# Opening of a two-sequence encoder layer on one core: inputs transposed on the host, twelve gate/up blocks begun instead of seven, the opening's order written out by hand

## The chip, the cores and the metric

The kernel runs on one core of one Trainium2 chip. The metric is the device time of one execution in microseconds; lower is better. All arithmetic is in fp32; where a matrix product is wanted at fp32 accuracy, the kernel splits each operand into a rounded part ("hi") and its remainder ("lo") and adds three matmuls (hi x hi, hi x lo, lo x hi).

## The reference

Two sequences of 512 tokens, `x_prompt` and `x_sample` (1 x 512 x 1024 each), go through the same encoder layer:

```python
def swiglu(x, w_gate, w_up, w_down):
    return (jax.nn.silu(x @ w_gate) * (x @ w_up)) @ w_down

x = x + 0.5 * swiglu(rms_norm(x, ffn1_norm), ffn1_w_gate, ffn1_w_up, ffn1_w_down)   # 1024 -> 2816 -> 1024
h = rms_norm(x, mix_norm)                  # then attention and mLSTM in parallel, gated, merged
x = x + merged @ w_out
x = x + 0.5 * swiglu(rms_norm(x, ffn2_norm), ffn2_w_gate, ffn2_w_up, ffn2_w_down)
y = rms_norm(x, final_norm)
```

`rms_norm(x, g)` divides each token's row by the root of its mean square and multiplies each column by `g`. The change concerns the first line only: how the first feed-forward (FFN) is begun.

## The kernel before

The two sequences share every weight, so the kernel multiplies both at once by a scheme with seven products where eight would be expected (as Strassen's). For the gate and up matrices of one FFN, the 1024 input columns are halved (lower `l`, upper `u`), and the 2816 outputs are cut into 22 blocks of 128 (`NF`). A block needs seven products, each 12 matmuls of 128x512 (4 slices of 128 input columns x 3 for hi/lo): `B11`, `B21`, `T1`, `T2_`, `T3`, `T4`, `B22`. The right-hand sides of `B11` and `B21` are the lower and upper half of the prompt alone; those of the other five are the sample's upper half and differences of halves of both sequences. The weights' sides are the block's gate weights (`gu_left_a`) and differences of gate and up weights (`gu_left_b`). Each side is split into hi and lo by one ScalarE (ACT) and one VectorE (DVE) instruction (`w_pair`, `put`).

A block can therefore be begun with the prompt alone: `gu_first` multiplies `B11`, copies the partial sum out, adds `B21`, and takes the silu. `Up.begin` does that ahead of time and parks the two results in DRAM (`kept`); `Up.rest` is the loop over all 22 blocks, which fetches parked results back (`resume`) or does `gu_first` itself, and then does the other five products (`gu_rest`). Before, `AHEAD = 7` blocks are begun, and `ORDER` alternates a begun block with one that is not, as long as there are begun ones:

```python
ORDER = [j for p in zip(range(AHEAD), range(AHEAD, NF)) for j in p] + list(range(2 * AHEAD, NF))
```

The opening before is this. Both sequences are loaded as rows (tokens on partitions, `load_x`). `norm_x(0)` squares and sums the prompt's rows on DVE, takes the reciprocal root in eleven small DVE instructions (`rstd_cols`, `rstd_of`), and divides the rows. TensorE then transposes the rows in 32 transposes of 128x128 (`turn`); from PSUM, `first_x` multiplies by the norm's gain `g1` and splits into hi and lo, and `park_x` writes the transposed prompt to DRAM (`xnbuf`) since PSUM and SBUF are wanted. Blocks 0 and 1 are begun, `norm_x(1)` and another 32 transposes do the same for the sample, `sums_of` and `right_sums` make the sums for the other five products, and blocks 2 to 6 are begun among them. Then comes `up.rest`, then the down projection (`ffn_down`).

A planner sets the order of the instructions on each engine from the order of the program and from priorities (`shifted`), except where `pin` (`tc.keep_in_program_order`) holds them in the written order. DMAs of the SP queue are issued in order, each after its own wait.

Of the kernel before, what the change touches and what calls it, by code (L numbers as in the profile page):

```python
# [8 lines left out]
F32 = mybir.dt.float32  # L9
# [17 lines left out]
def encoder(ctx, tc, I, outs):  # L27
# [97 lines left out]
    nc.gpsimd.dma_start(g1, I["ffn1_norm"][0].rearrange("(k p) -> p k", p=P))  # L125


# [5 lines left out]
    warm = cpool.tile([P, 1], F32, name="warm")  # L133
    nc.scalar.activation(warm, ones[:, 0:1], AF.Silu)
# [41 lines left out]
    def rstd_cols(v, width, n):  # L176
        a = rs_tile(width)
        nc.vector.tensor_scalar(a, v, 1.0 / n, EPS, op0=ALU.mult, op1=ALU.add)
        return rstd_of(a, width)

    def col_sums(acc, bs=(0, 1, 2, 3)):
# [4 lines left out]
        nc.vector.tensor_reduce(c, p[:, bs[0] * P:(bs[-1] + 1) * P].rearrange("p (b d) -> p b d", d=P), axis=AX.X,  # L186
                                op=ALU.add)
        return c

    def bcast_psum(r):  # L190

        pr = PT()
        for b in range(4):
            nc.tensor.transpose(pr[:, b * P:(b + 1) * P], r[:, b:b + 1].to_broadcast([P, P]), ident)
        return pr
# [51 lines left out]

    def w_pair(t, src, pin=lambda i: i):
        pin(nc.scalar.activation(t[:, 0], src, AF.Copy))  # L249
        pin(V_.tensor_tensor(t[:, 1], src, f(t[:, 0]), op=ALU.subtract))  # L250
# [13 lines left out]
    def gu_left_b(rg, ru, ring, left):  # L264
# [5 lines left out]
        V_.tensor_tensor(a, u0, u1, op=ALU.add)  # L270
        V_.tensor_tensor(u0, g0, u0, op=ALU.subtract)
        V_.tensor_tensor(g0, a, g0, op=ALU.subtract)
        V_.tensor_tensor(g1_, g1_, g0, op=ALU.subtract)
        wb = w8_tile()
        w_pair(wb, halves(rg))
        left.update({T2_: part(wb, 0), B22: part(wb, 1)})

        def more():
            wd = [v(ring.wd(F32R)) for _ in range(2)]
            split(a, *wd)  # L280
            wc = w8_tile()
            w_pair(wc, halves(ru))
# [3 lines left out]
    def product(p, w, xt, first):  # L286
        wh, wl = w
        for k in range(HK_):
            for i, (a, b) in enumerate(((wh, 0), (wh, 1), (wl, 0))):
                nc.tensor.matmul(p, a[:, k, :], xt[:, b, k, :], start=(first and k == 0 and i == 0),  # L290
                                 stop=(k == HK_ - 1 and i == 2), skip_group_check=True)
# [16 lines left out]
    def gu_rest(W, xc, got, ring, mid):  # L308

        Y, Z = PS(), PT()  # L310
        second = lambda: product(Y, W[T2_], xc[T2_], True)
# [61 lines left out]
    AHEAD = 7  # L373

    ORDER = [j for p in zip(range(AHEAD), range(AHEAD, NF)) for j in p] + list(range(2 * AHEAD, NF))

    class Up:


        def __init__(self, xc, wg, wu, rb):  # L380
            self.xc, self.rb = xc, rb
            self.v = wg, wu
# [13 lines left out]
            r.junk = [r.o.rows[1][:, i] for i in range(2)]  # L396
            r.lone, r.last = lone, fa
# [13 lines left out]
        def rest(self, raw, at=None, hook=None):  # L411
            ring = self.ring

            def resume(j):
                got = ring.v(), ring.h()
                for t, d in zip(got, self.kept.pop(j)):
                    nc.sync.dma_start(t[:, 0], d)
                return got

            left = {}  # L420
            gu_left_b(*raw, ring, left)()
            raw = self.fetch(ORDER[1])
            got = resume(ORDER[0])
            for i, j in enumerate(ORDER):
# [7 lines left out]
                h = gu_rest(W, self.xc, got, ring, lambda: then.append(resume(nxt)) if nxt in self.kept else None)  # L432
# [23 lines left out]
    def ffn_down(wd, rb, ring, tail, xres, done, at_step, hook, ends=None):  # L456
# [19 lines left out]
        def load_raw(fp, i):  # L476
# [3 lines left out]
            fb = ORDER[2 * fp + i]  # L480
# [135 lines left out]
    def mix_gains():  # L616
        pin = tc.keep_in_program_order
        for t, n in ((gm, "mix_norm"), (g2, "ffn2_norm")):
            pin(nc.gpsimd.dma_start(t, I[n][0].rearrange("(k p) -> p k", p=P)))
        pin(nc.gpsimd.dma_start(gbias, I["mlstm_gate_bias"].rearrange("a c -> (a c)").partition_broadcast(P)))  # L620
        pin(nc.gpsimd.dma_start(hn, I["mlstm_head_norm"][0].rearrange("(k p) -> p k", p=P)))
# [529 lines left out]
    raws = [A([P, 4, D], F32, "raw") for _ in range(2)]  # L1151
    xc = [None] * 7
    up = Up(xc, I["ffn1_w_gate"], I["ffn1_w_up"], rbuf[0])
    xins = [I[n][0] for n in ("x_prompt", "x_sample")]

    kept = [[dpool.tile([P, S], F32, name=f"kept{j}_{i}") for i in range(2)] for j in range(AHEAD)]

    def load_x(s):
        for b in range(4):
            nc.sync.dma_start(raws[s][:, b, :], xins[s][b * P:(b + 1) * P, :])  # L1160

    def turn(s, k, banks):
        p = banks[k % len(banks)]()
        for b in range(4):
            nc.tensor.transpose(p[:, b * P:(b + 1) * P], raws[s][:, b, k * P:(k + 1) * P], ident)
        return p
# [31 lines left out]
    def norm_x(s):  # L1198

        sq = [spool.tile([P, 4], F32, tag="cs4", bufs=4, name=nm("cs4")) for _ in range(2)]  # L1200
        junk = up.ring.junk
        for b in range(4):
            for i in range(2):
                x_ = raws[s][:, b, i * S:(i + 1) * S]
                pin(V_.scalar_tensor_tensor(junk[i], x_, 1.0, x_, op0=ALU.mult, op1=ALU.mult,
                                            accum_out=sq[i][:, b:b + 1]))
        pin(V_.tensor_tensor(sq[0], sq[0], sq[1], op=ALU.add))
        rs = rstd_cols(sq[0], 4, D)
        for b in range(4):
            if b % 2:  # L1210
                pin(nc.scalar.activation(raws[s][:, b, :], raws[s][:, b, :], AF.Copy, scale=rs[:, b:b + 1]))
            else:
# [279 lines left out]
```

## Time and profile before

| | |
|---|---|
| time, median of 3 runs | 2116.05 us (2113.82 to 2117.22) |
| profiled execution: its own time | 2115.01 us |
| profiled execution: span from first to last instruction | 2113.2 us |
| granted TensorE clock, mean | 0.996 |
| busy share of TensorE (PE) / its weight loads / DVE / ACT / GpSimd (POOL) | 98% / 80% / 74% / 45% / 5% |
| mean DMA rate | 170 GB/s |

In the profile, PE stands for TensorE's matmuls and PEld for its weight loads, SPq for the queue that issues most DMAs. Times in a timeline start at the span's first instruction. A row of several merged instructions gives the start of the first, the time to the end of the last, and their number; in square brackets stands the idle time of the engine before it and what ended it. Matmuls are pipelined: the pace is the distance of starts, not the duration of one.

### The profile page before, as it was taken

The numbers are of one execution on the slowest core, as the hardware profiler recorded it, in microseconds if no ns is written. First come the engines' busy times: TensorE is split into PE (matmuls) and PEld (weight loads), VectorE is DVE, ScalarE is ACT, GpSimd is POOL, SyncE is SP. The second block draws the span as 40 slices with busy tenths as digits, with TensorE's granted clock in tenths as the row PEclk, the third lists the DMA queues.
The fourth block names the chain that finished last, engine by engine and source line by source line (L and its number), as shares of the span: only waits on it lengthen the run. The fifth ranks groups of instructions, "written<-read, shape, count | busy, mean of one in ns | idle before, by whom it ended". The sixth has DMA issues, their size and how long they took to land.

```text
span 2113.2 us, 26221 instructions
## 1 busy us (share of the span) xinstructions
PE 2070.4 (98%) x9472; PEld 1694.7 (80%) x9472; DVE 1556.0 (74%) x2569; ACT 940.6 (45%) x1568; POOL 97.4 (5%) x106
## 2 busy tenths in 40 slices
PE   7999999999999999999999999999999999999997
PEld 5888888888888777878887787788788888888886
DVE  7888787776796796574649865764887877776687
ACT  6443443442225566463436555544543434343224
POOL 0000000001000110000101101010000000000002
PEclk9999999999999999999999999999999999999999
DMA  7464543389764222232341222344546544369763
GB/s 268 150 222 166 211 179 140 145 323 387 263 230 140 76 75 73 82 117 83 117 159 56 75 91 79 130 156 163 169 154 225 179 169 179 140 245 403 275 212 139
DMA packets 137489, 361.76 MB, mean 171 GB/s; under 512 B 13360, under 2 KB 13376, under 8 KB 136336
## 3 DMA queue, kind: packets, MB, share of 16 engines
q1 hardware_dynamic: 136480, 358.30, 47.7%
q0 software_dynamic: 592, 1.27, 0.3%
q8 instruction: 74, 1.21, 0.2%
q10 hardware_dynamic: 288, 0.52, 0.1%
q14 instruction: 55, 0.45, 0.1%
HBM read 255.15 MB, written 104.89 MB: 170 GB/s over the span
## 4 chain that ended last, share of the span: by engine, by line
PE 85%; DVE 7%; ACT 3%; DMA 3%; issue 1%; SPq 0%; POOL 0%; ACTq 0%; DVEq 0%; POOLq 0%
PE pss L290 17%; PE mm L696 14%; PE pst L290 11%; PE mm L290 10%; PE mm L540 7%; PE mm L680 4%; PE pst L540 4%; PE pss L540 4%; PE mm L1125 3%; PE pso L540 2%; PE pso L952 2%; PE pso L680 1%; PE pss L924 1%; PE pso L1081 1%; PE pss L1032 1%
## 5 line engine op out<-in xcount | busy, mean ns | idle before, releaser
L290 PE MATMUL pss<-xc,w 128*128 128x512 f32 x1584 | 379.4, 390 | 0.7 <-DVE t L320 0.7
L290 PEld LDWEIGHTS pss<-xc,w 128*128 128x128 f32 x1584 | 297.3, 188 | 63.1 <-DVE t L320 1.1
L696 PE MATMUL mm<-xh,w 128*128 128x512 f32 x896 | 293.6, 397 | 0.9 <-DVE w L212 0.9
L290 PE MATMUL mm<-xc,w 128*128 128x512 f32 x1056 | 254.4, 392 | 2.2 <-ACT f L299 2.1
L249 ACT ACTIVATE w<-wr 128x1024 fp32r<-128x1024 f32 x132 | 139.6, 1059 | 236.8 <-PE pst L290 143.6
L290 PEld LDWEIGHTS mm<-xc,w 128*128 128x128 f32 x1056 | 196.9, 188 | 46.3 <-ACT f L299 6.0
L212 DVE TENSOR_TENSOR w<-wr,w 128x1024 fp32r<-128x1024 f32 (+1 forms) x112 | 135.7, 1213 | 116.0 <-ACT w L211 114.9
L250 DVE TENSOR_TENSOR w<-wr,w 128x1024 fp32r<-128x1024 f32 x132 | 161.2, 1223 | 80.5 <-ACT w L249 80.0
L696 PEld LDWEIGHTS mm<-xh,w 128*128 128x128 f32 x896 | 167.8, 189 | 33.6 <-DVE w L212 1.3
L540 PE MATMUL mm<-w,rt 128*128 128x512 f32 x792 | 185.5, 390 | 0.3 <-DMA rt<-rbuf 0.3
L696 PE MATMUL mm<-xl,w 128*128 128x512 f32 x448 | 177.8, 397 | 0.0
L540 PEld LDWEIGHTS mm<-w,rt 128*128 128x128 f32 x792 | 148.5, 188 | 31.4 <-DMA rt<-rbuf 0.7
L211 ACT ACTIVATE w<-wr 128x1024 fp32r<-128x1024 f32 (+1 forms) x112 | 114.6, 1030 | 109.8 <-PE pso L1125 35.0
L290 PE MATMUL pst<-xc,f 128*128 128x512 f32 x528 | 127.2, 389 | 0.0
L290 PE MATMUL pst<-xc,w 128*128 128x512 f32 x528 | 127.0, 389 | 0.0
L290 PEld LDWEIGHTS pst<-xc,w 128*128 128x128 f32 x528 | 99.1, 188 | 20.6
L290 PEld LDWEIGHTS pst<-xc,f 128*128 128x128 f32 x528 | 99.1, 188 | 20.5
L600 ACT ACTIVATE w<-t 128x512 fp32r<-128x512 f32 x82 | 51.6, 631 | 121.9 <-PE pst L540 63.7
L600 ACT ACTIVATE w<-wr 128x512 fp32r<-128x512 f32 x72 | 44.7, 631 | 129.1 <-PE pso L540 65.5
L696 PEld LDWEIGHTS mm<-xl,w 128*128 128x128 f32 x448 | 84.7, 189 | 16.0
L540 PE MATMUL pss<-w,rt 128*128 128x512 f32 x396 | 95.3, 390 | 0.9 <-ACT w L600 0.9
L540 PE MATMUL pst<-w,rt 128*128 128x512 f32 x396 | 94.3, 389 | 0.0
(344 smaller groups left out, 3496.2 us busy)
## 6 DMA issues: line engine op xcount, KB each, us to landing
rt<-rbuf SPq DMA_DIRECT2D x154, 512.0 KB, 6.1
rbuf<-t SPq DMA_DIRECT2D x72, 512.0 KB, 3.2
wr<-in_ffn_w_gate_dram SPq DMA_DIRECT2D x56, 512.0 KB, 4.1
wr<-in_w_in_cols_dram SPq DMA_DIRECT2D x56, 512.0 KB, 3.5
wr<-in_ffn_w_up_dram SPq DMA_DIRECT2D x44, 512.0 KB, 3.5
rbuf<-f SPq DMA_DIRECT2D x30, 512.0 KB, 3.1
rbuf<-tab SPq DMA_DIRECT2D x30, 512.0 KB, 3.7
wr<-in_ffn_w_down_dram SPq DMA_DIRECT2D x48, 256.0 KB, 7.4
```

The costliest lines, as they stand in the source:

```text
L211: pin(nc.scalar.activation(hi, raw, AF.Copy))
L212: pin(lo_eng.tensor_tensor(lo, raw, f(hi), op=ALU.subtract))
L249: pin(nc.scalar.activation(t[:, 0], src, AF.Copy))
L250: pin(V_.tensor_tensor(t[:, 1], src, f(t[:, 0]), op=ALU.subtract))
L290: nc.tensor.matmul(p, a[:, k, :], xt[:, b, k, :], start=(first and k == 0 and i == 0), stop=(k == HK_ - 1 and i == 2), skip_group_check=True)
L540: nc.tensor.matmul(p, r[:, b, d * P:(d + 1) * P], u[:, a, :], start=(first and q == 0 and k == 0), stop=(q == len(us) - 1 and k == 2), ski ...
L600: nc.scalar.activation(hi, src, AF.Copy)
L680: nc.tensor.matmul(p[b][:, :N], a[:, k, bs], w_[:, kl, :], start=(k == 0 and i == 0), stop=(k == KD - 1 and i == 2))
L696: nc.tensor.matmul(p, a[:, k, :], b, start=(k == 0 and i == 0), stop=(k == n - 1 and i == 2))
L924: nc.tensor.matmul(p, qT[:, h, b * P:(b + 1) * P], kv[:, hk * 2 + j, :], start=(j == 0), stop=(j == 1))
L952: nc.tensor.matmul(po, Vst[:, kv_, hk, :], w, start=(kv_ == 0 and i == 0), stop=(kv_ == 3 and i == 1))
L1125: nc.tensor.matmul(p[b], a[:, k, bs], w_[:, k - k0, :], start=(k == 0 and i == 0), stop=(k == KD - 1 and i == 2))
```

## The change

The host hands the kernel each input twice: as rows, as before, and transposed (`x_prompt_t`, `x_sample_t`, 128 partitions x 8 slices x 512 tokens); the four norm gains that lie along partitions are laid out on the host too, as 128 rows. The 64 transposes of the opening and the trip of the prompt through `xnbuf` are gone there (the second FFN keeps its own `sums_of`).

Twelve blocks are begun in the first FFN, seven in the second (`RAW, AHEAD = 6, (12, 7)`). A token's divisor is the same for all input columns, so it can be applied after a product as well: blocks 0 to 5 are begun on the prompt times gain, not divided ("raw"), and their two results are multiplied on DVE by `R[0]`, a 128x512 tile that holds each token's reciprocal root in all partitions (`end`). Meanwhile the rows are squared and summed on ACT (`squares`), rooted on DVE (`root`), and spread over the partitions by four small TensorE transposes (`spread`). Then `normed` divides the transposed prompt, and blocks 6 to 11 are begun on it as before. The sample is divided likewise, half on DVE and half on POOL (`normed1`). Blocks come in pairs: the lower halves (`lower`) of two blocks, then their upper halves (`upper`); `evac` copies the partial sum out between the two.

Everything up to the first product of the loop is pinned in written order on every engine and on the SP queue; the first slice of the prompt goes over ACT's DMA queue. In the loop, the order is 0, 12, 1, 13, ... 9, 21, 10, 11, and the first block's weights are made in the opening.

```diff
-    g1 = ...; nc.gpsimd.dma_start(g1, I["ffn1_norm"][0].rearrange("(k p) -> p k", p=P))
...
-    AHEAD = 7
-    ORDER = [j for p in zip(range(AHEAD), range(AHEAD, NF)) for j in p] + list(range(2 * AHEAD, NF))
+    RAW, AHEAD = 6, (12, 7)
+    def order_of(ahead):
+        return [j for p in zip(range(ahead), range(ahead, NF)) for j in p] + (
+            list(range(2 * ahead, NF)) or list(range(NF - ahead, ahead)))
...
-    load_x(0)
-    raw0 = up.fetch(0, (0,))
-    load_x(1)
-    raw1 = [up.fetch(j, (0,))[0] for j in (1, 2)]
-    norm_x(0)
-    W = [gu_left_a(raw0[0], pin)]
...
-    for k in range(KD - 1):
-        first_x(k)
-    park_x(0)
-    first_x(KD - 1)
-    W.append(gu_left_a(raw1[0], pin))
-    up.begin(0, W[0])
-    for k in range(1, KD):
-        park_x(k)
-    up.begin(1, W[1])
-    norm_x(1)
...
+    load_x(0, 0, 1, nc.scalar)
+    load_half(0, 0)
+    pin(nc.sync.dma_start(g1, I["ffn1_norm"]))
...
+    load_x(0, 1, 2)
+    load_x(0, 2, 4)
+    load_half(1, 0)
+    load_half(0, 1)
+    load_x(0, 4, 6)
+    load_x(0, 6, 8)
+    load_half(1, 1)
+    raws = {2: fetch_next(2)}
+    load_rows(0, (0, 1))
+    raws[3] = fetch_next(3)
+    load_rows(0, (2, 3))
...
+    def split_x(k):
+        t, kk, g, x = xr[k // HK_], k % HK_, g1[:, k:k + 1], x_t[0][:, k, :]
+        pin(nc.scalar.activation(t[:, 0, kk, :], x, AF.Copy, scale=g))
+        pin(V_.scalar_tensor_tensor(t[:, 1, kk, :], x, g, f(t[:, 0, kk, :]), op0=ALU.mult, op1=ALU.subtract))
+    def squares(s, b):
+        v = in_rows[:, b, :]
+        pin(nc.scalar.activation(v, v, AF.Square, accum_out=row_sq[s][:, b:b + 1]))
+    def root(s):
+        return rstd_cols(row_sq[s], 4, D, pin)
+    def spread(s, r):
+        pin(nc.scalar.activation(R[s], bcast_psum(r, pin), AF.Copy))
+    def normed(ks):
+        for k in ks:
+            x = x_t[0][:, k, :]
+            pin(V_.scalar_tensor_tensor(x, x, g1[:, k:k + 1], R[0], op0=ALU.mult, op1=ALU.mult))
...
+    def end(j):
+        X, v1 = begun.pop(j)
+        up.kept[j] = kept[j]
+        if j < RAW:
+            g0 = gate_rows()
+            pin(V_.tensor_tensor(g0, X, R[0], op=ALU.mult))
+            pin(V_.tensor_tensor(v1, v1, R[0], op=ALU.mult))
+            pin(nc.scalar.activation(g0, g0, AF.Silu))
+            pin(nc.sync.dma_start(kept[j][0], v1))
+        else:
+            g0 = part_rows()
+            pin(nc.scalar.activation(g0, X, AF.Silu))
+        pin(nc.sync.dma_start(kept[j][1], g0))
...
+    first_left(0, 0)
+    for k in range(HK_):
+        split_x(k)
+    lower(0)
+    first_left(1, 0)
+    first_left(0, 1)
+    split_x(4)
+    split_x(5)
+    evac(0)
+    lower(1)
+    split_x(6)
+    split_x(7)
+    first_left(1, 1)
+    upper(0)
+    evac(1)
+    upper(1)
+    left(2)
+    squares(0, 0)
+    squares(0, 1)
+    left(3)
+    lower(2)
+    squares(0, 2)
+    squares(0, 3)
+    lower(3)
+    evac(2)
+    fetch_more(4, 5)
+    for k in range(0, KD, 2):
+        load_x(1, k, k + 2)
+    fetch_more(6, 7)
+    load_rows(1, range(4))
+    left(4)
+    r = root(0)
+    upper(2, (0, 1))
+    evac(3)
+    spread(0, r)
+    upper(2, (2, 3))
+    upper(3)
+    left(5)
+    fetch_more(8, 9)
+    normed(range(4))
+    lower(4)
+    lower(5)
+    hi_all(B11, x0l)
+    lo6 = left_hi(6)
+    end(0)
+    evac(4)
+    normed(range(4, 8))
+    hi_all(B21, x0u)
+    upper(4)
...
+    lower(10)
+    lower(11)
+    evac(10)
+    more = gu_left_b(*raw0, rings, W0, pin)
+    hi_all(T1, x0l)
+    upper(10)
+    evac(11)
+    upper(11)
+    lo_all(T1, x0l)
+    more()
+    end(10)
+    end(11)
+    pin(V_.tensor_tensor(x1l, x1u, x1l, op=ALU.subtract))
+    both(T3, x1l)
+    sum2(t4s, lambda i: two(x0u, i), lambda i: t2s[i])
+    both(B22, x1u)
+    both2(T4, t4s)
...
-    tail = up.rest(raw0, 13, mix_gains)
+    tail = up.rest(raw0, 13, mix_gains, W0)
...
+    for n in ("prompt", "sample"):          # on the host
+        x = given[f"x_{n}"][0]
+        given[f"x_{n}_t"] = np.ascontiguousarray(x.T.reshape(KD, P, S).transpose(1, 0, 2))
+    for name in ("ffn1_norm", "mix_norm", "ffn2_norm", "mlstm_head_norm"):
+        given[name] = np.ascontiguousarray(given[name][0].reshape(-1, P).T)
```

More of the change, by code (lines that the diff above doesn't have):

```diff
@@ new lines, in encoder @@
+    first_left(0, 0)
+    for k in range(HK_):
+        split_x(k)
[24 more added lines that the diff above has]
+        load_x(1, k, k + 2)
@@ new lines, in encoder @@
+    squares(1, 0)
+    squares(1, 1)
+    squares(1, 2)
+    lo8 = left_hi(8)
+    squares(1, 3)
+    end(1)
+    lower(6)
+    lower(7)
+    evac(6)
+    end(2)
+    lo8()
+    gain1(range(HK_, KD))
+    lo9 = left_hi(9)
+    evac(7)
+    r = root(1)
+    end(3)
+    upper(6, (0, 1))
+    spread(1, r)
+    lo9()
+    normed1()
+    upper(6, (2, 3))
+    upper(7)
+    end(4)
+    end(6)
+    lo10 = left_hi(10)
+    pin(V_.tensor_tensor(x0l, x1l, x0l, op=ALU.subtract))
+    lower(8)
+    end(7)
@@ new lines, in encoder @@
+    lower(9)
+    lo10()
+    evac(8)
+    upper(8)
+    lo11 = left_hi(11)
+    evac(9)
+    upper(9)
+    end(5)
+    lo11()
+    raw0 = up.fetch(up.order[0])
+    sum2(t2s, lambda i: two(x1u, i), lambda i: two(x0l, i))
+    end(8)
+    W0 = {}
+    both2(T2_, t2s)
+    end(9)
+    lower(10)
[11 more added lines that the diff above has]
+    pin(V_.tensor_tensor(x1l, x1u, x1l, op=ALU.subtract))
```

234 lines of the change are left out of this document (141 added, 93 removed).

## The prediction

> **What bounds the kernel now.** I read the page first, for where TensorE stands still.
>
> ```profile
> PE 2070.4 (98%) x9472; PEld 1694.7 (80%) x9472; DVE 1556.0 (74%) x2569; ACT 940.6 (45%) x1568; POOL 97.4 (5%) x106
> PE   7999999999999999999999999999999999999997
> ```
>
> TensorE is busy 98% of the span, so 43 us is all the idle time there is. The first slice of 53 us, one of two that are not full, is where the change lies. So I asked for the opening by windows, with the loop behind it.
>
> ```profile
> 0.00:10.00 10.00, 3.78 (x16) 3.49 (x16) 4.12 (x14) 1.49 (x2) 4.84 (x11) 1.00 0.81 224
> 10.00:20.00 10.00, 4.39 (x23) 4.16 (x24) 6.82 (x21) 5.29 (x7) 0.23 (x1) 1.00 1.01 394
> 20.00:30.00 10.00, 9.21 (x46) 7.38 (x45) 9.91 (x21) 9.55 (x17) 0.00 (x0) 1.00 0.53 209
> 30.00:40.00 10.00, 7.07 (x32) 5.79 (x31) 7.91 (x25) 5.52 (x7) 0.00 (x0) 0.83 0.90 312
> 40.00:450.00 410.00, 410.00 (x1817) 339.17 (x1816) 330.66 (x412) 177.30 (x231) 0.00 (x0) 1.00 0.51 183
> ```
>
> The columns are PE, PEld, DVE, ACT and POOL busy, granted clock, DMA share and GB/s. After 40 us TensorE is full to 450 us (410.00 of 410), with DVE at 81%. Before that 15.5 us are idle, and part of the busy time is not products. What the opening costs in all comes from TensorE's timeline.
>
> ```profile
> 15.61 0.78 PE L1165 MATMUL pss<-ident,raw 128*128 128x128 f32 x2 [10.79 <-DVE raw L1213]
> 17.46 1.06 PE L1165 MATMUL pss<-ident,raw 128*128 128x128 f32 x4
> 19.17 1.14 PE L1165 MATMUL mm<-ident,raw 128*128 128x128 f32 x8
> 20.50 2.57 PE L290 MATMUL mm<-xc,w 128*128 128x512 f32 x10
> 23.25 0.71 PE L290 MATMUL mm<-xc,w 128*128 128x512 f32 x2
> 24.76 5.76 PE L290 MATMUL mm<-xc,w 128*128 128x512 f32 x24 [0.79 <-ACT f L299]
> 31.25 3.03 PE L290 MATMUL mm<-xc,w 128*128 128x512 f32 x12 [0.73 <-ACT f L299]
> 36.48 0.48 PE L1165 MATMUL pss<-ident,raw 128*128 128x128 f32 x1 [2.20 <-DVE raw L1213]
> 39.81 3.46 PE L290 MATMUL mm<-xc,w 128*128 128x512 f32 x14
> 44.12 3.02 PE L290 MATMUL mm<-xc,w 128*128 128x512 f32 x12
> 47.55 13.99 PE L290 MATMUL mm<-xc,w 128*128 128x512 f32 x60
> 61.37 0.62 PE L290 MATMUL pss<-xc,w 128*128 128x512 f32 x2
> 77.48 2.88 PE L290 MATMUL pst<-xc,w 128*128 128x512 f32 x12
> 80.20 2.88 PE L290 MATMUL pss<-xc,w 128*128 128x512 f32 x12
> ```
>
> The pace of products is (80.20 - 77.48)/12 = 0.2267 us. Until 61.37, 10 + 2 + 24 + 12 + 14 + 12 + 60 = 134 matmuls of products were started, worth 30.4 us. So 61.37 - 30.4 = 31.0 us of the opening brought no product: the wait for the rows' norm, 64 transposes, the second norm. The change leaves the number of products alone (22 blocks x 84 matmuls = 1848, or 419 us at this pace), so the difference in time is the difference in this lost time, as long as TensorE stays full afterwards.
>
> **The change part by part: the lost time after it.** The price rows for the other engines:
>
> ```profile
> 0.72 1.82 SPq L1160 DMA_DIRECT2D raw<-in_x_prompt_dram  x4
> 1.24 1.10 POOL L125 DMA_DIRECT2D g<-in_ffn_norm_dram  x1 [0.81 <-POOLq L1479]
> 4.29 0.69 DVE L1205 SCALAR_TENSOR_TENSOR tab<-raw 128x512 f32<-128x512 f32 x1 [3.29 <-DMA raw<-in_x_prompt_dram]
> 12.52 0.17 DVE L178 TENSOR_SCALAR rs<-cs 128x4 f32<-128x4 f32 x1
> 14.71 2.19 ACT L1211 ACTIVATE raw<-raw,rs 128x1024 f32<-128x1024 f32 x2 [12.49 <-DVE rs L173]
> 17.75 0.66 ACT L1228 ACTIVATE xc<-pss,g 128x512 fp32r<-128x512 f32 x1
> 18.32 0.67 ACT L1228 ACTIVATE xc<-pst,g 128x512 fp32r<-128x512 f32 x1
> 19.02 0.75 DVE L1229 SCALAR_TENSOR_TENSOR xc<-pss,g,xc 128x512 fp32r<-128x512 f32 x1
> 19.68 0.74 DVE L1229 SCALAR_TENSOR_TENSOR xc<-pst,g,xc 128x512 fp32r<-128x512 f32 x1
> 24.12 0.59 ACT L299 ACTIVATE f<-mm 128x512 f32<-128x512 f32 x1
> ```
>
> ```profile
> L249 ACT ACTIVATE w<-wr 128x1024 fp32r<-128x1024 f32 x132 | 139.6, 1059 | 236.8 <-PE pst L290 143.6
> L250 DVE TENSOR_TENSOR w<-wr,w 128x1024 fp32r<-128x1024 f32 x132 | 161.2, 1223 | 80.5 <-ACT w L249 80.0
> ```
>
> *First product: 5.5 us.* The first 512 KB of the prompt, issued at 0.72, were there at 4.29. After the change the first 512 KB are one prompt slice (ACT's queue) and half of block 0's weights (SP's), so 4.3 again. ACT splits the half weight and the slice at 0.57 to 0.6 each: first matmul at 5.5. The norm, the transposes and `xnbuf` are on nobody's path now.
>
> *First product held by DVE: 0.5.* DVE makes five lo parts at 0.66 (19.02 to 19.68), from 4.95 to 8.3, and two matmuls follow: 8.7 instead of 5.5 + 2.7 = 8.2.
>
> *Clock: 2.1.* Four transposes from 17.46 to 18.31 came at 0.21 each, but eight from 19.17 at 0.14: TensorE had been still for 10.8 us and reached its pace some 3.5 us after it began at 15.61. The same pace of 0.21 returned where the record grants 0.54:
>
> ```profile
> 8.00:10.00 2.00, 0.00 (x0) 0.00 (x0) 1.31 (x4) 0.00 (x0) 0.00 (x0) 1.00 1.05 202
> 12.00:14.00 2.00, 0.00 (x0) 0.00 (x0) 1.69 (x11) 0.00 (x0) 0.23 (x1) 1.00 1.03 416
> 18.00:20.00 2.00, 2.00 (x14) 2.00 (x13) 2.00 (x3) 2.00 (x4) 0.00 (x0) 1.00 1.01 403
> 38.00:40.00 2.00, 2.00 (x12) 2.00 (x11) 1.16 (x2) 2.00 (x3) 0.00 (x0) 0.54 0.87 311
> ```
>
> (The 1.00 ahead of the first row is then no grant, only the absence of a record.) No row shows a slow 128x512; I estimate twice 0.2267. If the full clock comes 5 us after the first product, at 10.5, the twelfth matmul starts near 10.4 and ends the product at 10.8 instead of 8.7. Bounds: 0 (full clock from the start) and 3.5 (3 us later still). The Trainium skill, "TensorE: Matmul & The Clock Gate", Part 1, says that the clock runs at half until a free-running window of about 3.4 us has been busy throughout. By that alone full clock comes 3.4 to 6.8 us after 5.5, which makes this term 1.4 to 3.2. The transposes' 3.5 us agree.
>
> *First spread: 1.1.* TensorE reaches the four transposes of `spread` 18 matmuls after `lower(2)` (12 of `lower(3)`, 6 of `upper(2)`), or 4.1 us. In that time runs a chain that `lower(2)` starts, since ACT and DVE go in written order: `evac(2)` 0.6, `left(4)` on ACT 1.06, on DVE 1.22, then `root`, eleven small instructions, 14.71 - 12.52 = 2.2: 5.1, and handovers, 5.2. So TensorE waits 1.1 wherever it stands. Queued behind it are `upper(2)`'s second half and all later products; on DVE `normed`, whose cover is the four raw blocks still to multiply. Bounds 0.5 to 3.5: `squares` needs the prompt's rows, the last of 6 MiB on the queue. At 403 GB/s these land at 4.3 + 5.77 MB/403 = 18.6, and two squares and a weight split later ACT is free by 21, before `lower(2)` is over: the slack is 1 to 2 us, and below about 360 GB/s this wait grows.
>
> *Second spread: 0.* `root(1)` comes after `squares(1)`, whose rows are there by 4.3 + 12.1 MB/403 = 34.3, and before TensorE arrives: 174 matmuls after 10 us of losses, near 50.
>
> *Eight spread transposes:* at 0.14, 1.1, against 64 removed.
>
> *Other waits: 0.4.* DVE has about 40 instructions of 512 columns (0.66), 21 of 1024 (1.22; the 2048-wide ones count twice) and two roots (4.4) ahead of `T2_`: 56 us of the 71 up to 76 us. So the engine isn't the bound; a late handover costs 0 to 4, and I take 0.4, near the timeline's small waits (0.73, 0.79).
>
> *The loop: 0.* TensorE needs (1848 - 288) x 0.2267 = 354 us for what was 381. DVE had 81% of 381 = 307; five more blocks are begun, so five splits of 1.22 leave the loop: 301 of 354, 85%. The cover is thinner, not gone. Ten more fetches of 256 KB go at a DMA share of 0.51. The last pair (10, 11) has two begun blocks, 27.2 us of TensorE against 26 of DVE: the tightest place, price 0 to 2.
>
> *Gains on POOL's queue:* later and contiguous, needed only after the loop: 0.
>
> Sum: 5.5 + 0.5 + 2.1 + 1.1 + 1.1 + 0.4 = 10.7 lost, instead of 31.0: 20.3 saved. The profiled execution's own time is 2115.0 (span 2113.2 and 1.8 around it), so 2094.7; the median of the runs is 1.0 above that execution: 2096.
>
> **The rivals.** *The queue is too slow (slower).* Ahead of the second loop block's weights, SP's queue carries 20.75 MiB, 21.8 MB: both sequences twice (8), twelve gate blocks (6), four loop weights (2), nineteen parked results (4.75). They are wanted by 78 us; that is 287 GB/s from 2 us on. Everything is pinned, so a late piece stops ACT or DVE and, behind it, every product. Pure loads made 403 to 416 (against); mixed with stores, 312 at a DMA share of 0.90, so some 347 (against, with little to spare); but 202 at 8 to 10 us (for), with the small gain DMAs in flight that POOL issued from 1.24 on and that are gone here. At 202 the list ends at 110 us, 32 late: 2128. It decides below 287, and at 227 the gain is gone. The Trainium skill, "DMA: Bandwidth & Descriptors", asks for transfers of 1 MiB or more (section "Measured (HBM→SBUF, 128 partitions, SWDGE, issued from GpSimd)") and gives a single one 2.0 us plus its bytes at 436 GB/s ("Anatomy of one DMA", for POOL's path); one at a time, pieces of 512 KB would by that make 164 GB/s and 2151. The rows of 403 and 416, of such pieces with several in flight, speak against it.
>
> *The clock falls back.* The record's 0.54 came right after 2.2 us of idle time (36.48). If the waits at the first spread and at 5 us do the same, another 3.4 us at half pace: 1.7 each, 2098 to 2100.
>
> *DVE is late at `T3`.* After `T2_`'s sides DVE still has T1's lo, a weight and a 2048-wide difference, T3's lo and smaller ones, 11.7 us, against 7.7 us of products that don't need them (T2_, T1, ten matmuls). It leads by some 4 us when `T2_` starts; without the lead, 4 us are lost: 2100.
>
> *The change doesn't do what it says* is excluded by the built order: the 64 transposes are gone, the products stand in the written order (chance 0).
>
> **How the numbers follow.** The forecast (2091 to 2099): 0.72. Low end: no clock term, no wait at the spread, 3.6 less than 10.7, and half a microsecond from an earlier landing: 2091. The clock falling back: 0.08, DVE late: 0.05, the queue at 255 to 285 GB/s (up to 10 late): 0.07; together 2099 to 2107, 0.20. The queue lower: 0.08, of which 0.03 still faster, 0.02 within 0.2% (4.2 us, about what a measurement can tell from no change), 0.03 slower. Faster 0.95, same 0.02, slower 0.03; range 2091 to 2107.
>
> **What would show it.** Right: first product at 5 to 6 us; block 0's twelve matmuls over 4 to 5.5 us; about 1 us of idle time at `spread` for DVE's `root`, none at the second; the first `T2_` matmul 288 x 0.2267 + 10 to 11 = 75 to 77 us in; TensorE full until the down projection. Wrong: idle time before `upper` or `lower` that ends with a DMA landing or with ACT after one; a DMA rate under 300 GB/s at a full share in the first 70 us; new waits in the loop.

## The result, and the profile after

| | before | after |
|---|---|---|
| median of the runs compared | 2114.94 us (2113.54 to 2117.22, 4 runs) | 2098.03 us (2094.34 to 2100.79, 4 runs) |
| profiled execution: time / span | 2115.01 / 2113.2 us | 2100.79 / 2099.0 us |

The ratio is 0.9918, with a 95% interval of 0.9899 to 0.9937: faster by 17 us. The forecast was 2096 us (2091 to 2107), so the time is 2 us above it. The direction and most of the size were right, but the profile shows that one step of the sum was not.

TensorE's busy share by slices, from the page of the kernel after:

```profile
PE   9999999999999999999999999999999999999997
```

The first digit of TensorE's line went from 7 to 9: the opening is where the time came from. The windows of the kernel after, with the columns as before (PE, PEld, DVE, ACT, POOL busy, granted clock, DMA share, GB/s):

```profile
0.00:10.00 10.00, 7.03 (x24) 5.46 (x25) 3.66 (x8) 5.57 (x9) 0.68 (x6) 0.92 0.77 250
10.00:20.00 10.00, 10.00 (x42) 8.16 (x41) 6.64 (x10) 9.26 (x15) 0.00 (x0) 0.91 1.03 412
20.00:30.00 10.00, 9.02 (x43) 7.24 (x42) 3.46 (x13) 5.06 (x9) 0.00 (x0) 1.00 1.03 411
30.00:40.00 10.00, 10.00 (x45) 8.06 (x44) 9.91 (x13) 6.06 (x7) 0.00 (x0) 1.00 0.87 345
40.00:50.00 10.00, 10.00 (x46) 8.29 (x45) 9.66 (x20) 10.00 (x18) 0.00 (x0) 1.00 0.60 208
50.00:60.00 10.00, 10.00 (x48) 8.23 (x47) 9.74 (x10) 3.49 (x7) 7.20 (x5) 1.00 0.63 215
60.00:70.00 10.00, 8.13 (x29) 6.19 (x29) 9.65 (x10) 7.07 (x11) 2.97 (x5) 0.83 0.86 264
70.00:80.00 10.00, 9.70 (x43) 7.73 (x42) 8.42 (x10) 6.22 (x9) 0.00 (x0) 1.00 0.64 239
80.00:430.00 350.00, 350.00 (x1545) 289.33 (x1544) 299.71 (x382) 146.85 (x187) 0.00 (x0) 1.00 0.58 202
```

Two things stand out. From 60 to 70 us TensorE is idle for 1.9 us and the granted clock is 0.83, in a stretch for which the forecast had no loss. And DVE, with 13.8 us of work in the first 30 us, is then busy for 39.0 of 40.

TensorE's timeline of the kernel after, up to the first matmul of `T2_` (the one at 80.98), and the start of the down projection:

```profile
6.24 0.50 PE L289 MATMUL mm<-xc,w 128*128 128x512 f32 x1 [1.42 <-ACT xc L1245]
22.64 2.88 PE L289 MATMUL pso<-xc,w 128*128 128x512 f32 x12
25.36 1.52 PE L289 MATMUL mm<-xc,w 128*128 128x512 f32 x6
27.86 0.62 PE L189 MATMUL pst<-ident,rs 128*128 128x128 f32 x4 [0.98 <-DVE rs L168]
28.24 1.63 PE L289 MATMUL mm<-xc,w 128*128 128x512 f32 x6
50.30 0.60 PE L189 MATMUL pst<-ident,rs 128*128 128x128 f32 x4
57.56 2.88 PE L289 MATMUL pso<-xc,w 128*128 128x512 f32 x12
62.31 4.61 PE L289 MATMUL mm<-xc,w 128*128 128x512 f32 x12 [1.87 <-ACT t L1281]
66.76 2.91 PE L289 MATMUL pso<-xc,w 128*128 128x512 f32 x12
69.50 8.32 PE L289 MATMUL mm<-xc,w 128*128 128x512 f32 x36
78.13 3.02 PE L289 MATMUL mm<-xc,w 128*128 128x512 f32 x12 [0.30 <-ACT f L1281]
80.98 2.88 PE L289 MATMUL pss<-xc,w 128*128 128x512 f32 x12
434.91 1.30 PE L543 MATMUL mm<-w,rt 128*128 128x512 f32 x5
```

The start of the down projection in the kernel before:

```profile
450.12 2.20 PE L540 MATMUL mm<-w,rt 128*128 128x512 f32 x9
```

The twelve begun blocks have 24 matmuls each. These 288 matmuls at 0.2267 us are 65.3 us, so 80.98 - 65.3 = 15.7 us were lost ahead of the loop, where 10.7 were forecast and 31.0 were lost before. The down projection began at 450.12 before and begins at 434.91 now: 15.2 us saved, and the loop kept them.

Most of the 5 us that are missing stands at one place. The twelve matmuls at 62.31 (`upper(8)`) could have started at 57.56 + 2.72 = 60.28. They started 2.0 us later, and then took 4.45 us (62.31 to 66.76) instead of 2.72, 1.7 more, because the record grants half the clock for 3.4 us from 62.9 on. Another 0.5 us is lost ahead of 78.13. TensorE waited for ACT's `evac(8)`. What ACT waited for before that, by the waits of the kernel after (total, times, longest):

```profile
ACT tab L1295 <- DVE tab L1293: 7.1, 2, 6.5
```

ACT stood 6.5 us in `end(4)`, behind DVE. In the written order three other ACT operations stand between `end(4)`'s silu and `evac(8)`. What DVE did at that time, by its timeline in the kernel after:

```profile
52.75 5.84 DVE L1344 SCALAR_TENSOR_TENSOR xt<-xt,g,tab 128x512 f32<-128x512 f32 x4 [0.26 <-ACT tab L1256]
58.52 0.68 DVE L1293 TENSOR_TENSOR tab<-pss,t 128x512 f32<-128x512 f32 x1
59.12 1.18 DVE L1294 TENSOR_TENSOR t<-t,t 128x512 f32<-128x512 f32 x1
```

POOL's timeline:

```profile
52.80 6.94 POOL L1347 TENSOR_TENSOR xt<-xt,tab 128x512 f32<-128x512 f32 x4 [51.51 <-ACT tab L1256]
```

DVE's groups from 30 to 66 us (busy us, mean ns of one):

```profile
L1344 DVE SCALAR_TENSOR_TENSOR xt<-xt,g,tab 128x512 f32<-128x512 f32 x4 | 5.8, 1519 | 0.3 <-ACT tab L1256 0.3
L1261 DVE SCALAR_TENSOR_TENSOR xt<-xt,g,t 128x512 f32<-128x512 f32 x8 | 5.5, 747 | 0.0
```

L1344 and L1261 are the same operation on tiles of the same shape. L1261 (`normed`, nothing beside it) takes 747 ns; L1344 (`normed1`, beside POOL's L1347) takes 1519 on average and as a group 5.84 us instead of 2.73. That is 3.1 us by which DVE reaches `end(4)` late. L1293, which takes one operand from PSUM, was not slower beside POOL (0.68); L1294, with both operands in SBUF, was (1.18 instead of 0.68), though it reads neither of the tiles that POOL reads. ACT has a smaller part: it puts the gains on POOL's four slices (`gain1`, 2.56 us) ahead of the copy that hands DVE the spread root, and DVE waited 0.26 us for that copy.

So the theory: *POOL's half of `normed1` slows DVE's half; ACT, in its written order, stands behind DVE, and TensorE behind ACT; the clock falls back behind that wait.* The rivals: DVE is slow there for another reason (its operands, transfers that land); ACT is late by its own work; the losses at the start (clock, spread) matter more.

### The profile page after: what moved, and what is told of

Its sections match the earlier page's. It is cut to its first block, busy times and chain, and to the rows that moved or that the text cites. A ratio compares the mean times of both kernels' runs of the same rounds, so it can differ in the third digit from the quotient of the medians.

```text
span 2099.0 us, 26135 instructions
## 1 busy us (share of the span) xinstructions
PE 2064.2 (98%) x9416; PEld 1687.8 (80%) x9416; DVE 1567.0 (75%) x2554; ACT 942.4 (45%) x1571; POOL 106.6 (5%) x109
## 4 chain that ended last, share of the span: by engine, by line
PE 89%; DVE 6%; ACT 3%; DMA 1%; issue 1%; POOL 0%; SPq 0%; ACTq 0%; DVEq 0%; POOLq 0%
PE pss L289 18%; PE mm L699 15%; PE pst L289 11%; PE mm L289 9%; PE mm L543 8%; PE pst L543 4%; PE pss L543 4%; PE mm L683 4%; PE mm L1128 3%; PE pso L543 3%; PE pso L955 2%; PE pso L683 1%; PE pss L927 1%; PE pso L1084 1%; PE pss L1035 1%; PE pso L1128 1%
## 5 line engine op out<-in xcount | busy, mean ns | idle before, releaser
L289 PE MATMUL pss<-xc,w 128*128 128x512 f32 x1632 | 389.4, 389 | 0.0
L289 PEld LDWEIGHTS pss<-xc,w 128*128 128x128 f32 x1632 | 306.1, 188 | 64.3 <-ACT t L1281 0.3
L248 ACT ACTIVATE w<-wr 128x1024 fp32r<-128x1024 f32 (+1 forms) x129 | 134.8, 1046 | 245.0 <-PE pst L289 131.4
L289 PE MATMUL mm<-xc,w 128*128 128x512 f32 x960 | 234.2, 395 | 4.7 <-ACT t L1281 1.9
L207 DVE TENSOR_TENSOR w<-wr,w 128x1024 fp32r<-128x1024 f32 (+1 forms) x112 | 136.3, 1218 | 116.6 <-ACT w L206 116.0
L289 PEld LDWEIGHTS mm<-xc,w 128*128 128x128 f32 x960 | 181.2, 190 | 46.8 <-ACT f L298 2.9
L249 DVE TENSOR_TENSOR w<-wr,w 128x1024 fp32r<-128x1024 f32 (+1 forms) x129 | 155.5, 1206 | 81.7 <-ACT w L248 81.2
L206 ACT ACTIVATE w<-wr 128x1024 fp32r<-128x1024 f32 (+1 forms) x112 | 114.6, 1030 | 110.2 <-PE pso L1128 35.0
```

Of the source, the lines that this page charges most:

```text
L206: pin(nc.scalar.activation(hi, raw, AF.Copy))
L207: pin(lo_eng.tensor_tensor(lo, raw, f(hi), op=ALU.subtract))
L289: pin(nc.tensor.matmul(p, a[:, k, :], xt[:, b, k, :], start=(first and k == 0 and i == 0), stop=(k == HK_ - 1 and i == 2), skip_group_chec ...
```

## The experiments

The wait that some expectations place at "the fifth divided block" is the one ahead of `upper(8)`; the one that they place at the end of the opening, at 77 us, is the wait of `upper(11)` for `evac(11)`.

**The changed kernel again.** No edit.

> The changed kernel again, unaltered, on the same chip as the runs beside it. Expected 2096 to 2100 us, as in the result (2094.3 to 2100.8 there). If the spread there came from whether the clock's fall-back at 62.9 us happens in an execution, a profile of a shorter execution shows full clock at 62 to 66 us, or a shorter wait ahead of it; if the spread has nothing to do with that stall, the profile shows the stall of about 2 us and the clock at half behind it at any length.

2099.60 us (2097.20 to 2100.32, 5 runs), ratio 0.9925 [0.9913, 0.9938]. The same wait of 1.84 us at 62.86 and the same 4.5 us for the twelve matmuls behind it, `T2_` from 81.50 on. The wait is a property of the kernel, not of one execution. The profiled execution was again the slowest of its runs, so it doesn't tell what makes the spread among them.

**`normed1` on DVE alone.**

```diff
-    def normed1():
-        for k in range(HK_):
+    def normed1(ks=range(KD)):
+        for k in ks:
...
-        for k in range(HK_, KD):
-            x = x_t[1][:, k, :]
-            pin(G_.tensor_tensor(x, x, R[1], op=ALU.mult))
...
-    gain1(range(HK_, KD))
```

> The second sequence's normalisation wholly on VectorE: all eight slices there, GpSimd's four products and the gains that ScalarE put on them are gone. Theory (VectorE's 128x512 operations took 1.77 us instead of 0.75 because GpSimd read and wrote beside them): the eight take 0.75 each, 6 us, so VectorE, though it has twice the work, is through at about 58.7 us, as it was with half of it; the wait of 2 us ahead of the fifth divided block's lower product stays within 1 us of that, and the time within 2 us of the changed kernel's. Rival (the operations are slow for another reason: their operands, the transfers that land beside them): they stay at 1.5 to 1.8 us, the eight take 12 to 14, VectorE is 6 to 8 us later and the kernel 4 to 8 us slower than the changed one.

2095.62 us (2095.06 to 2096.22), 4.0 less than the changed kernel beside it. DVE's group from 30 to 66 us:

```profile
L1344 DVE SCALAR_TENSOR_TENSOR xt<-xt,g,tab 128x512 f32<-128x512 f32 x8 | 5.4, 747 | 0.0
```

TensorE's timeline:

```profile
61.26 3.02 PE L289 MATMUL mm<-xc,w 128*128 128x512 f32 x12 [1.03 <-ACT t L1281]
78.57 2.88 PE L289 MATMUL pss<-xc,w 128*128 128x512 f32 x12
```

Eight divisions alone take 5.4 us, less than four beside POOL (5.84), so the rival of other operands or landings falls. The time went further than expected ("within 2 us"): the wait shrank from 1.87 to 1.03 us, and no half clock followed it. Only about half of these 0.84 us is the contention. The divisions end 0.46 us sooner for their duration, and they begin some 0.4 us sooner after the second spread (52.14 - 50.08 against 52.75 - 50.30), because the edit also takes `gain1` off ACT. The down projection starts at 432.63, against 434.91 and 435.45 in the two executions of the changed kernel: 2.3 to 2.8 us earlier. What the medians show beyond that arose later.

**The upper half of `normed1` later.** The edit above, and:

```diff
-    normed1()
+    normed1(range(HK_))
...
     raw0 = up.fetch(up.order[0])
+    normed1(range(HK_, KD))
     sum2(t2s, lambda i: two(x1u, i), lambda i: two(x0l, i))
```

> As the run with the normalisation wholly on VectorE, and the upper four slices are divided later, just ahead of the difference that first needs them. Theory (contention with GpSimd, and ScalarE waiting for VectorE in the written order, made the wait of 2 us and the half clock of 1.7 us behind it): VectorE leaves the first four slices at about 55.8 us instead of 58.6, the wait ahead of the fifth divided block and the half clock at 62.9 to 66.3 us go, 3 to 3.7 us faster than the changed kernel beside it; 3 us of work come later on VectorE, so a wait of up to 2.4 us can come back at the last two lower products, which leaves 1 to 2 us of gain. Rival (ScalarE is late by its own work, VectorE's lateness is only beside it): the wait stays at 1.9 us and the time within 0.5 us.

2097.73 us (2097.15 to 2100.26). TensorE's timeline:

```profile
60.13 2.88 PE L289 MATMUL mm<-xc,w 128*128 128x512 f32 x12
76.26 4.50 PE L289 MATMUL mm<-xc,w 128*128 128x512 f32 x12 [2.37 <-ACT f L1281]
```

The wait at `upper(8)` is gone, without half clock; the one at `evac(11)` came back at its full 2.4 us with a half clock behind it (4.33 us to the next product). Both as expected, and so is the gain, 1.9 us less than the changed kernel beside it. ACT's silu in `end(4)` now waits 3.87 us for DVE instead of 6.51. So it was DVE that made ACT late; ACT's own work had no more than the 0.4 us above, since `gain1` is gone here too.

**Also `evac(11)` ahead of the next weight split.** The two edits above, and:

```diff
     evac(10)
-    more = gu_left_b(*raw0, rings, W0, pin)
     hi_all(T1, x0l)
-    upper(10)
     evac(11)
+    more = gu_left_b(*raw0, rings, W0, pin)
+    upper(10)
     upper(11)
```

> As the run before it (upper four slices divided on VectorE, later), and ScalarE evicts the last begun block ahead of the next block's weight split, which is put behind it, with the last two upper products later. Theory: both waits at the end of the opening are gone, the first product of the second loop pair's operand starts at 77 to 78 us instead of 81, and the kernel is 3 to 5 us faster than the changed kernel beside it. Rival (the loop has no room for what is put off: the weight split and the upper slices come later): the first loop product is early, but waits of 2 to 4 us show in the first loop blocks, and the time is within 1 us of the changed kernel's.

2096.39 us (2094.49 to 2097.07), 3.2 less than the changed kernel. Both waits are gone. TensorE's timeline:

```profile
24.32 2.88 PE L289 MATMUL pso<-xc,w 128*128 128x512 f32 x12
67.40 11.04 PE L289 MATMUL mm<-xc,w 128*128 128x512 f32 x48
78.28 2.88 PE L289 MATMUL pss<-xc,w 128*128 128x512 f32 x12
```

`T2_` begins at 78.28, later than it would have, since in this execution the first 60 matmuls (five half products) lasted until 24.32 instead of 22.64: the half clock lasted 6.8 us there instead of 3.4. The rival has a part too: two waits for DVE appear in the loop, of 0.60 us at 84.94 and of 0.69 at 95.16. From `T2_` to the down projection 355.9 us pass instead of 353.9, so the down projection starts only 0.7 to 1.3 us earlier than in the changed kernel (434.19).

**Longer warm-up.** `for _ in range(8)` becomes `range(11)`: 22 warm-up matmuls instead of 16.

> The changed kernel with 22 warm-up matmuls of 128 columns instead of 16 ahead of the first product (11 passes of two instead of 8), so that TensorE stands still for less than the 1.2 to 1.4 us it does there. Theory (the loss of 2.8 to 4.8 us between the first product's start and the end of the first five half products is the clock, and which window of 3.4 us is busy throughout depends on its phase): full clock comes from the first product on in more executions, the 60 matmuls take 14.5 to 16.5 us instead of 16.4 to 18.4, the kernel is 0 to 2 us faster. Rival (these matmuls wait for VectorE's and ScalarE's splits of late slices, whatever the clock): the 60 matmuls take the same 16.4 or more and the time is the same.

2098.20 us (2097.91 to 2098.64). TensorE's timeline:

```profile
5.97 0.56 PE L289 MATMUL mm<-xc,w 128*128 128x512 f32 x1
21.35 2.88 PE L289 MATMUL pso<-xc,w 128*128 128x512 f32 x12
61.05 3.06 PE L289 MATMUL mm<-xc,w 128*128 128x512 f32 x12 [1.88 <-ACT t L1281]
77.49 4.61 PE L289 MATMUL mm<-xc,w 128*128 128x512 f32 x12 [2.50 <-ACT f L1281]
81.94 2.90 PE L289 MATMUL pss<-xc,w 128*128 128x512 f32 x12
```

The first 60 matmuls took 15.4 us instead of 16.4, with no half clock among them, so the forecast's clock term is real. Yet `T2_` starts no earlier (81.94), and the time is that of the changed kernel (its ratio to the kernel before is 0.9919; the changed kernel's were 0.9918 and 0.9925). The lead of 1.3 us was still there behind the first wait for ACT (61.05 against 62.31), and no half clock followed that wait. All of it was lost at the second wait, 2.50 us for `evac(11)`, and at the half clock behind it.

**The gains on the host, in the kernel before.** The kernel before, with `g1` on SP's queue and all four gains contiguous.

> The kernel before, with only the four gains laid out on the host: the first on SyncE's queue, the others contiguous on GpSimd's queue. Theory of the prediction's queue rival (the 202 GB/s at 8 to 10 us came from the small gain transfers in flight): the rate at 4 to 10 us rises towards 400, the prompt's last rows land 2 to 3 us sooner, the norm and all behind it with them, 2 to 3 us faster than before (ratio 0.9986 to 0.9990). Rival (the transfers start slowly whatever is small beside them): the rate at 8 to 10 us stays near 200 and the time within 0.5 us.

2115.10 us (2112.80 to 2118.43); ratio 1.0000 [0.9991, 1.0009]. Windows of this kernel:

```profile
6.00:8.00 2.00, 0.00 (x0) 0.00 (x0) 1.49 (x6) 0.00 (x0) 0.00 (x0) 1.00 1.08 228
8.00:10.00 2.00, 0.00 (x0) 0.00 (x0) 0.82 (x3) 0.00 (x0) 0.40 (x1) 1.00 0.92 351
```

At 8 to 10 us the rate rose from 202 to 351 GB/s, but the dip only moved, to 228 at 6 to 8 us. Expected was 2 to 3 us; it was nothing that can be measured. The scattered gains did not cause the slow start, and this part of the change is worth nothing by itself.

**The prompt's root ahead of block 4's weight.** `r = root(0)` is written ahead of `left(4)`.

> The changed kernel with the prompt's root written ahead of block 4's weight split instead of behind it. Prediction's step (TensorE waits 1.1 us at the first spread because evacuation, weight split and root follow one another on VectorE): the wait of 1.0 us ahead of the first spread goes, 1 us earlier from there on; the weight of block 4 comes 2.2 us later and is not wanted before 18 matmuls more. The time is 1 us less if nothing later waits for another reason, and up to 0.5 us less if VectorE's lateness at the fifth divided block (which does not change) takes the rest back. Rival (the squares, so the queue, are what comes late): the wait stays.

2099.12 us (2097.40 to 2099.91). TensorE's timeline:

```profile
26.84 1.52 PE L289 MATMUL mm<-xc,w 128*128 128x512 f32 x6
28.20 0.60 PE L189 MATMUL pst<-ident,rs 128*128 128x128 f32 x4
78.51 4.61 PE L289 MATMUL mm<-xc,w 128*128 128x512 f32 x12 [1.95 <-ACT f L1281]
```

The wait of 1.0 us at the first spread is gone (26.84 + 6 x 0.2267 = 28.20), so it was the order on DVE, as forecast, and not the rows' transfers. The time is the changed kernel's (ratio 0.9921). Two things took the gain: in this execution the half clock at the start lasted longer (the first 60 matmuls took 18.1 us instead of 16.4), and `evac(11)` was waited for again, with half clock behind it.

**Seven blocks begun instead of twelve.** `RAW, AHEAD = 6, (7, 7)`, and what blocks 7 to 11 did in the opening left to the loop.

> The changed kernel with seven blocks begun in the first feed-forward network instead of twelve: six on undivided input and one on divided input; blocks 7 to 11 are left to the loop. Theory (the twelve blocks are the cover for VectorE's opening; without five of them TensorE stands still until the first difference of the four input quarters is made): 120 matmuls, 27 us, less cover, 5 weight splits and evictions less on VectorE and ScalarE, so a wait of 15 to 20 us ahead of the first loop product, 2112 to 2120 us, which is the kernel before again. Rival (VectorE's opening is mostly the work of the blocks themselves): the wait is under 8 us and the time under 2106.

2120.68 us (2118.58 to 2123.97); ratio 1.0024 [1.0014, 1.0033], slower than before. TensorE's waits:

```profile
PE pss L289 <- ACT w L248: 20.9, 1, 20.9
```

One wait of 20.9 us, ahead of the first `T2_` product; expected were 15 to 20, and 2112 to 2120 us. The five more blocks are the cover for DVE's opening. The same early start, without them, gains nothing at all.

**All four edits together** (sample's division on DVE in two halves, `evac(11)` early, root early, 22 warm-up matmuls).

> Four edits of the changed kernel together: the sample's normalisation wholly on VectorE with its upper half later, the last eviction ahead of the weight split, the prompt's root ahead of block 4's weight split, 22 warm-up matmuls. Theory (each of the last two brought TensorE 1 us or more forward and lost it again to the two waits of ScalarE for VectorE and SyncE's queue at 61 and 77 us; with those waits gone it is kept): first loop product at 73.5 to 76 us, 9 to 10.5 us lost ahead of it, 2092 to 2095 us, 3 to 6 us faster than the changed kernel. Rival (the waits at 61 and 77 us are the limit of all the opening's work on VectorE, so what is brought forward is lost again in another wait): first loop product at 77 us or later, and the time that of the run with the first two edits, 2096.

2095.82 us (2094.33 to 2097.17). TensorE's timeline:

```profile
75.73 2.88 PE L289 MATMUL pss<-xc,w 128*128 128x512 f32 x12
431.81 6.28 PE L543 MATMUL mm<-w,rt 128*128 128x512 f32 x27
```

`T2_` starts at 75.73, with 75.73 - 65.3 = 10.4 us lost: near the 10.7 that the forecast had for the change, but by another sum. The wait at the first spread is gone, while the start cost 9.3 us where the forecast had 5.5 + 0.5 + 2.1. The clock stayed full here too, but ACT waited 0.83 and 1.60 us for slices of the prompt to land, and the first 60 matmuls took 16.9 us. Kept until the down projection are 3.1 us against the changed kernel (434.91 to 431.81), since 2.1 us are lost in the loop (356.1 us from `T2_` to the down projection instead of 353.9), where waits for DVE of 0.56 and 0.75 us appear. The time missed its range by 0.8 us and can't be told from that of the run with the division on DVE alone (2095.62) or with the first two of these edits (2096.39).

**POOL beside DVE elsewhere.** In the changed kernel, four POOL products ahead of `normed(range(4))`:

```diff
+    for _ in range(4):
+        pin(G_.tensor_tensor(R[1], R[0], R[0], op=ALU.mult))
     normed(range(4))
```

> The changed kernel with four more GpSimd products of 128x512 (the reciprocal root's tile squared into the tile that the sample's root is written to later, so no result is changed) beside the first four divisions of the prompt on VectorE. Theory (two engines share the way to the on-chip memory): VectorE's divisions, 0.75 us each in every run so far, take 1.7 to 1.8 for as long as GpSimd works beside them, 3 to 4 us in all; VectorE has no idle time behind it until 60 us, so TensorE meets it as a wait at the sixth block or at the eighth: 2 to 4 us slower than the changed kernel. Rival (only the sample's tiles, or gains read beside them, are slow): 0.75 us as before and the same time.

2100.80 us (2099.13 to 2101.46). DVE's timeline, then POOL's:

```profile
31.26 5.08 DVE L1261 SCALAR_TENSOR_TENSOR xt<-xt,g,t 128x512 f32<-128x512 f32 x4
```

```profile
29.22 5.91 POOL L1396 TENSOR_TENSOR tab<-t 128x512 f32<-128x512 f32 x4 [27.93 <-ACT t L1256]
```

TensorE's timeline:

```profile
40.29 5.74 PE L289 MATMUL pss<-xc,w 128*128 128x512 f32 x24 [2.24 <-ACT t L1281]
65.81 4.61 PE L289 MATMUL mm<-xc,w 128*128 128x512 f32 x12 [2.99 <-ACT t L1281]
437.95 0.84 PE L543 MATMUL mm<-w,rt 128*128 128x512 f32 x3
```

The very divisions that took 2.73 us in every other run take 5.08, though nothing that they read or write has changed. POOL had begun 2 us ahead of DVE (29.22 to 35.13), so 2.4 us were added and not the 3 to 4 expected. TensorE meets them at once, as a wait of 2.24 us ahead of `upper(4)`, and then waits longer ahead of `upper(8)` (2.99 instead of 1.87). The down projection starts 3.0 us later than in the changed kernel: there is no slack behind DVE in this stretch. The median is 1.2 to 2.8 us above that kernel's two medians, where 2 to 4 were expected, but the intervals of the ratios overlap (0.9919 to 0.9946 here, 0.9913 to 0.9938 for the changed kernel run again), so this is read from the timeline and not from the time.

**The runs side by side** (all but the one with seven blocks). Lost time ahead of the loop in the profiled executions, in us: from the span's start to the end of the first 60 matmuls, less their 13.6 (start); at the first spread; and all other waits, with the half clock behind them. The eight spread transposes are 0.7 in each.

| | start | first spread | other waits | `T2_` starts | down projection starts |
|---|---|---|---|---|---|
| kernel after | 9.0 | 1.1 | 4.8 | 80.98 | 434.91 |
| the same again | 9.6 | 1.1 | 4.8 | 81.50 | 435.45 |
| `normed1` on DVE alone | 8.8 | 1.1 | 2.6 | 78.57 | 432.63 |
| its upper half later | 8.9 | 1.1 | 4.5 | 80.59 | 434.69 |
| also `evac(11)` early | 10.7 | 1.1 | 0.4 | 78.28 | 434.19 |
| longer warm-up | 7.7 | 1.1 | 7.0 | 81.94 | 435.74 |
| root early | 10.5 | 0 | 6.4 | 82.95 | 436.84 |
| all four edits | 9.3 | 0 | 0.4 | 75.73 | 431.81 |
| POOL beside `normed` | 9.1 | 1.1 | 7.8 | 84.02 | 437.95 |

As long as DVE and `evac(11)` stay where they are, what is saved at the start or at the spread comes back under other waits. The rival that the start mattered more falls by the same sum: in the kernel after the start cost 9.0 us, where 8.1 were forecast, and the other waits 4.8, where 0.4 were.

## Why the prediction was right, and where it was wrong

- **The unit of account held.** Lost time ahead of the loop fell from 31.0 to 15.7 us; the down projection starts 15.2 us earlier, and the medians differ by 16.9. That the median came out only 2 us above the forecast is in part luck. The forecast's 10.7 us of lost time belong to 2094.7 us in the profiled execution; measured were 15.7 and 2100.79, 6 us more. The forecast put the median 1.0 us above the profiled execution; it lies 2.8 below, since the one profiled is the slowest of its four.
- **First product: 5.5 forecast, 6.24 measured.** ACT's timeline of the kernel after shows that it waited for the first half weight until 4.94 us, where the forecast took 4.3 from a landing in the profile of before; why it came later stays open.

```profile
4.94 0.63 ACT L248 ACTIVATE w<-wr 128x512 fp32r<-128x512 f32 x1 [2.29 <-DMA wr<-in_ffn_w_gate_dram]
```

- **Held by DVE and clock: 2.6 forecast, 2.8 measured** (22.64 - 6.24 - 60 x 0.2267). Other executions gave 1.8 (longer warm-up) to 4.8 (the run with half clock for 6.8 us), 0.8 beyond 0.5 + 3.5, the forecast's hold and the upper bound of its clock term. The sum fits; the split isn't shown. DVE was not what held the first product: it waited 0.45 and 0.47 us for ACT there, and ACT waited 0.48 and 0.50 us for slices to land.
- **First spread 1.1 forecast, 1.1 measured; second 0 and 0.** Eight transposes took 0.7 instead of 1.1. The run with the root earlier shows the chain behind the first to be as forecast.
- **Other waits: 0.4 forecast, 4.8 measured.** This is the step that failed: "So the engine isn't the bound; a late handover costs 0 to 4, and I take 0.4". DVE's sum was right: 61.1 us up to 80 us, of which 3.6 came from the slowdown beside POOL, against 56 forecast. But 56 of 71 us is an average over two stages. DVE can't do its share until the norm is known; it had 13.8 us of work in the first 30 us and 39.0 in the next 40. In that second stage there is no slack, and any delay of DVE goes through ACT's written order to TensorE. Some 2 us of the delay came from a price that was not looked for at all: that POOL's half of `normed1` slows DVE's half. With that half on DVE, and its gains off ACT, the term is 2.6 us instead of 4.8. What is left of it is the lack of slack itself: with the upper half of the division and the next weight split put off as well, it is 0.4, as forecast, but then 2 us come back in the loop.
- **The rival "the clock falls back"** (0.08) happened, but behind this wait, not the one at the first spread; with 1.7 us, it was sized right. **"DVE is late"** (0.05) happened at block 8, not at `T3`. Together they cost what was expected of either, 2098 to 2100.
- **The queue rival** is refuted as what decides the time, by the rates (412 and 411 GB/s from 10 to 30 us). One of its signs did show, early and briefly: at 6 to 8 us the rate was 285 GB/s at a DMA share of 0.95, and the first matmuls waited for ACT, which waited for landings. The evidence held for it, that the gains' small transfers caused the 202 GB/s, was wrong: they are gone there, and a dip is not.
- **The loop: 0** held: TensorE full for 350.00 of 350 us, DVE at 299.71 (86%, 85% forecast).

The Trainium skill states the rule that speaks against `normed1`. "SBUF — State Buffer", section "Who interferes with whom", says that a VectorE instruction with two SBUF inputs contends with a GpSimd instruction that reads SBUF, and that one with at most one SBUF input, outside the two-port modes, does not. The trace agrees: 747 ns became 1519 on average, and 1779 at most, for two SBUF inputs, while L1293, with one operand in PSUM, stayed at 0.68 us beside POOL.

## What to carry to other kernels

Before giving half of an elementwise job to a second engine, price both halves running together: here DVE alone did eight slices in 5.4 us, and DVE and POOL together took 6.9, with 2.56 us of gains on ACT besides. Judge an engine's room stage by stage and from the moment its inputs exist, since "56 of 71 us" hid a stretch of 39.0 of 40. And when something is brought forward in a written order, follow it to the next engine that is full: the microsecond won by a longer warm-up in one run, and the one won by an earlier root in another, did not reach the loop, and in the run with all four edits, without the waits behind it, the earlier root's did.

## What the runs showed of the hardware that was not expected

Waits of TensorE of about 2 us sufficed for half clock: 1.84, 1.87, 1.95, 2.37, 2.50 and 2.99 us were each followed by some 3.4 us of it; others of 1.88, 1.89 and 2.24 us were not, nor were those near 1.0. Length alone does not decide it between 1.8 and 2.5 us. The Trainium skill, "TensorE: Matmul & The Clock Gate", section "Why this matters for your kernels", asks for no idle gaps above about 3 us. The runs here differ: waits of 1.84 us already cost 1.7 us of half clock.

The clock at the start differed with the warm-up. With 16 warm-up matmuls TensorE stood still for 1.2 to 1.5 us ahead of the first product, and in seven of eight such profiled executions the record grants half the clock during the first 60 matmuls, for 3.4 to 6.8 us; the eighth (the changed kernel again) has no half clock on record, but its 60 matmuls took 17.2 us without a wait, 3.6 more than at full pace. With 22 no such stop is in the timeline, and in both such executions the record grants the full clock throughout. Whether the stop or the length of the warm-up decides it isn't shown.

Half clock behind a wait also shows outside the change. From the start of the first to the start of the last of the L927 matmuls, some 490 us of the mixer which no edit touched, the ten profiled executions of the kernel after and its variants took 489.8 to 493.4 us. Two windows there, first of the kernel after, then of the run with `evac(11)` early:

```profile
1182.00:1186.00 4.00, 3.83 (x10) 3.02 (x11) 4.00 (x9) 2.89 (x9) 2.17 (x1) 0.57 0.40 131
```

```profile
1182.00:1186.00 4.00, 4.00 (x23) 2.98 (x22) 3.76 (x11) 2.54 (x6) 0.00 (x0) 1.00 0.28 105
```

At a clock of 0.57, TensorE ran 10 matmuls in these 4 us instead of 23. In both kernels a wait of over 2 us precedes (2.34 and 2.48). This alone moves an execution by more than some of the edits here, which is why the start of the down projection, not the time, was read for the smaller ones.
